# The start of a feed-forward stage in a hand-written order, two group sums in another group, and a two-factor multiply in the last norm

## The chip, the cores and the metric

The kernel runs on one core of a Trainium2 chip. The metric is device time in microseconds (us) of one execution; lower is better. All engines of the core (TensorE or PE, VectorE or DVE, ScalarE or ACT, GpSimd or POOL, and SyncE's queue SP for transfers) run side by side and wait for each other by semaphores.

## What is computed

One decoder block in float32 on 512 tokens of width 1024. The part that matters here is its second half:

```
x   = x + y @ W_out                              # 1024 x 1024
hm  = RMSNorm(x) * g_mlp
x   = x + relu(hm @ W1)**2 @ W2                  # W1 1024 x 4096, W2 4096 x 1024
out = RMSNorm(x) * g_final
```

Ahead of it stand a norm, an input projection, a pooling mixer, a latent attention with 8 heads and two gates. The change touches none of them.

## The kernel before

Every float32 matrix product is made of three matmuls on halves: an operand is cast by ScalarE to a rounded type (the high half, `hi`), VectorE subtracts that from the operand (the low half, `lo`), and TensorE adds hi*hi, hi*lo and lo*hi in PSUM. So each weight block costs a load, a ScalarE cast of 128x1024 and a VectorE subtraction of 128x1024 before TensorE can use it. Line 929 is the cast, line 932 the subtraction.

The feed-forward runs in four groups (`q` = 0 to 3) of 1024 hidden units. In each group both products are done in a form with seven block products where eight would be usual, at the price of sums and differences of blocks. In the "up" half (`up`, two halves `d` of 256 columns each) the seven block products are A11, S1, S2, A12, S3, S4 and A22, in this order on TensorE; S1 to S4 are running sums of weight blocks (`summed`, line 940). The tokens' side has the blocks B11, B21, B22 and the row forms T1 to T4, differences of blocks (`row_form`, lines 845 to 849, cast at line 1223, low half at line 1224). The results of S2 and S3 are copied to other PSUM banks before more is added (the forks `c` and `v`, line 1059; `b` at line 837 in group 0). ScalarE and VectorE then make relu squared and the forms of the hidden units (lines 1067 to 1092). In the "down" half (`down`) seven products, each in two steps, are added into the residual `xa` or into two kept sums, `U` and `V5` (line 1122). `U` and `V5` collect over groups 0 to 2 and are added to `xa` once, with eight VectorE additions of 128x512, at the end of `down` for group 2 (lines 1194 to 1201).

The order of all this is set by a small planner in the kernel's own Python (`emit_all`). Each operation has an engine, an assumed duration, the operations it needs, the buffers it takes, and a rank. The planner keeps an assumed clock for each engine (`free`). Time and again it takes, for each engine, the operations that could start within 0.2 us of the earliest one, chooses the one of lowest rank, and emits the choice that starts first. TensorE and SP take their lists strictly in order. On the chip each engine then runs its emitted list in order, and waits where an input is late. Weight blocks pass through five load buffers (`raw0` to `raw3` and `X`) and four pairs of hi and lo buffers.

Group 0 is special: its A11 and A12 are emitted by hand while W_out ends. The residual is norm'ed by 128-token tiles (`norm_rows`): tile 3 comes last, is transposed on TensorE into PSUM, and copied to `mT` (line 813), from which the row forms are made, for the first 128 columns of a block (`T[0, i]`) and for the last 128 (`T[1, i]`). In between, `early_forms` emits the weight sums S1 and S2 with their casts. Then the planner starts, from an assumed clock:

```python
    free.update(P=12.4, A=9.0, V=10.0)
    ...
    emit_all()
```

At the end the last norm squares each tile on ScalarE (`row_square`, line 1403), GpSimd raises the mean to the power -1/2 (line 1394), VectorE multiplies by `g_final` (lines 1427, 1428, 1443, 1446), and ScalarE (line 1410) or, for tile 3, VectorE (lines 1451, 1453) multiplies by the row's factor, half a row at a time, each half followed by its store on SP's queue. The last product's last tile is done in two halves of 256 columns.

Of the kernel before, what the change touches and what calls it, by code (L numbers as in the profile page):

```python
# [48 lines left out]
def block_kernel(ctx: ExitStack, tc: tile.TileContext, x, positions, g_mix, w_in, b_gate,  # L49
# [895 lines left out]
    def weights_up(q, d):  # L945
# [24 lines left out]
        rank_now[0] = step_of[K("S4")]  # L970
        s4 = summed(X("21"), X("21"), X("12"), p2 + [s3, ld["12"]])
        prepare(K("S4"), X("21"), [s4], 4)
        prepare(K("A22"), X("22"), [ld["22"]], 4)

# [32 lines left out]
    def up(q, d):  # L1007
# [25 lines left out]
        for n in UP_ORDER:  # L1033
# [19 lines left out]
            mm[n] = mm_op((q, d, n), UP_US, run, needs, (Bk[x],), (Bk[x],) if fresh else ())  # L1053
            if n in forks:
# [5 lines left out]
                fork_op[new] = use(act(512, copy, [mm[n]], step_of[q, d, n], (Bk[new],)), Bk[new], Bk[old])  # L1060
# [58 lines left out]
    given, r_op = [], {}  # L1119
# [7 lines left out]
    def down(q):  # L1127
# [158 lines left out]
    z = {n: [o for o in all_ops if o.tag == (0, 0, n)] for n in ("S1", "S2", "S3")}  # L1286
# [31 lines left out]
    def early_forms():  # L1318
        for o in z["S1"][1:] + z["S2"]:
            emit(o)  # L1320
# [47 lines left out]
    T = row_ops  # L1368
    def rows_then(*what):
        for o in what:  # L1370
            emit(o)
    rows_then(T[0, 0][0], T[0, 0][1], T[0, 1][0], T[0, 0][2], T[0, 1][1], T[0, 2][0], T[0, 1][2], T[0, 2][1], T[0, 3][0],
              T[0, 2][2], T[0, 3][1], T[0, 3][2])
# [4 lines left out]
    S3f = z["S3"]  # L1378
# [47 lines left out]
    for t in (0, 1):  # L1426
        nc.vector.tensor_mul(rows_o[t][0], xa[:, t, :], gf)
# [57 lines left out]
```

## Time and the profile before

| | |
|---|---|
| median of 3 runs | 684.94 us (684.65 to 686.38) |
| the profiled execution | 685.97 us |
| its span, first to last instruction | 684.2 us |
| TensorE busy, of the span | 663.0 us (97%) |
| VectorE, ScalarE, GpSimd busy | 516.0, 376.5, 83.2 us |
| mean granted TensorE clock | 0.991 of full speed |

The span is what the rows below are measured in; 1.77 us of the execution's own time lie around it. Times in rows count from the span's start. A timeline row gives start, duration, engine, line, operation, output<-input, shape and count; the square bracket at its end is how long the engine had been idle before it, and what ended the wait.

### The profile page before, as it was taken

To read this page: it belongs to the slowest core of one execution; us is meant where nothing else is said; L and a number is where in the kernel's file an instruction comes from. 1 tells how busy PE (TensorE), PEld (TensorE's weight loads), DVE (VectorE), ACT (ScalarE), POOL (GpSimd) and SP (SyncE) were. 2 spreads that over 40 slices of the span, in tenths; PEclk is the share of its full clock that TensorE was granted. 3 is DMA by queue.
4 is the path that set the end of the run, shared out by engine and by line. 5 is a ranking of instruction groups with operands and counts; after the bars stand their busy time and mean duration, and the time that the engine had idled before them with its cause. 6 is when DMAs were issued, how large, how long until landed. Compare 5 with 4: busy or idle time off the path is not lost.

```text
span 684.2 us, 9775 instructions
## 1 busy us (share of the span) xinstructions
PE 663.0 (97%) x3681; PEld 570.0 (83%) x3681; DVE 516.0 (75%) x793; ACT 376.5 (55%) x613; POOL 83.2 (12%) x101
## 2 busy tenths in 40 slices
PE   6999999999999999999998999999999999999994
PEld 3888888888888888888888977899889988899883
DVE  5767852478788764564579989788987989799996
ACT  4545252446655544442267784488535874368735
POOL 2216600000000000000000212002200022001212
PEclk8999999999999999999999999999999999999998
DMA  7423354642221125747504679338973398444953
GB/s 274 139 62 94 95 152 129 174 128 63 69 69 47 47 93 186 224 130 233 166 0 125 174 170 238 96 123 183 215 188 122 95 215 174 135 154 140 231 92 124
DMA packets 87047, 95.24 MB, mean 139 GB/s; under 512 B 6468, under 2 KB 61528, under 8 KB 87000
## 3 DMA queue, kind: packets, MB, share of 16 engines
q1 hardware_dynamic: 78296, 77.84, 36.1%
q0 software_dynamic: 8704, 16.78, 14.5%
q8 instruction: 29, 0.48, 0.3%
q14 instruction: 18, 0.15, 0.1%
HBM read 88.31 MB, written 6.29 MB: 138 GB/s over the span
## 4 chain that ended last, share of the span: by engine, by line
PE 89%; DVE 5%; ACT 2%; issue 1%; DMA 1%; POOL 0%; SPq 0%; POOLq 0%; DVEq 0%; ACTq 0%
PE P L777 7%; PE P L778 7%; PE P L776 7%; PE b L826 6%; PE a L826 5%; PE c L826 3%; PE v L826 3%; PE u L421 3%; PE lat L353 3%; PE e L826 2%; PE wo L777 2%; PE ga L71 2%; PE gb L70 2%; PE ga L70 2%; PE wo L776 2%; PE ga L72 2%
## 5 line engine op out<-in xcount | busy, mean ns | idle before, releaser
L929 ACT CAST xhi<-r_X 128x1024 fp32r<-128x1024 f32 x84 | 88.1, 1051 | 68.8 <-PE P L778 25.7
L932 DVE TENSOR_TENSOR xlo<-r_X,xhi 128x1024 fp32r<-128x1024 f32 x84 | 102.5, 1222 | 20.8 <-ACT xhi L929 20.3
L777 PE MATMUL P<-xlo,rhi 128*128 128x512 f32 (+1 forms) x228 | 89.5, 392 | 1.6 <-DVE xlo L932 1.5
L778 PE MATMUL P<-xhi,rlo 128*128 128x512 f32 (+1 forms) x228 | 89.1, 391 | 0.0
L776 PE MATMUL P<-xhi,rhi 128*128 128x512 f32 (+1 forms) x228 | 89.1, 391 | 0.0
L65 ACT CAST whi<-raw 128x1024 fp32r<-128x1024 f32 x45 | 46.7, 1050 | 45.4 <-PE bm L71 17.2
L66 DVE TENSOR_TENSOR wlo<-raw,whi 128x1024 fp32r<-128x1024 f32 x45 | 55.3, 1234 | 18.7 <-ACT whi L65 17.5
L777 PEld LDWEIGHTS P<-xlo,rhi 128*128 128x128 f32 x228 | 42.7, 187 | 12.7 <-DVE xlo L932 2.9
L776 PEld LDWEIGHTS P<-xhi,rhi 128*128 128x128 f32 x228 | 42.7, 187 | 10.0
L778 PEld LDWEIGHTS P<-xhi,rlo 128*128 128x128 f32 x228 | 42.7, 187 | 10.0
L915 POOL DMA_DIRECT2D r_X<-in_w_mlp_out x24 | 29.1, 1210 | 120.9 <-DVE xlo L932 116.6
L940 DVE TENSOR_TENSOR r_X<-r_X,r_X 128x1024 f32<-128x1024 f32 x32 | 39.1, 1223 | 5.0 <-DMA r_X<-in_w_mlp_in 4.5
L1081 DVE TENSOR_TENSOR rlo<-F,rhi 128x512 fp32r<-128x512 f32 x56 | 37.6, 687 | 6.9 <-ACT rhi L1078 6.8
L1078 ACT CAST rhi<-F 128x512 fp32r<-128x512 f32 x56 | 33.3, 620 | 1.0 <-DVE F L1087 0.5
L1122 DVE TENSOR_TENSOR xa<-xa,P 128x512 f32<-128x512 f32 (+1 forms) x53 | 33.0, 672 | 0.7 <-PE P L778 0.7
L665 ACT ACTIVATE p<-s,nm 128x128 f32<-128x128 f32 (+3 forms) x32 | 16.9, 528 | 19.9 <-DVE nm L662 19.4
L915 POOL DMA_DIRECT2D r_T<-in_w_mlp_out x8 | 9.7, 1213 | 145.3 <-ACT rhi L1078 49.5
L826 PE MATMUL a<-mb_hi,xhi 128*128 128x256 f32 x96 | 27.0, 281 | 0.0
L826 PE MATMUL a<-mb_hi,xlo 128*128 128x256 f32 x96 | 27.0, 281 | 0.0
L826 PE MATMUL a<-mb_lo,xhi 128*128 128x256 f32 x96 | 27.0, 281 | 0.0
L70 PE MATMUL gb<-h_hi,whi 128*128 128x512 f32 x64 | 26.4, 412 | 0.0
L71 PE MATMUL gb<-h_lo,whi 128*128 128x512 f32 x64 | 25.6, 400 | 0.0
(297 smaller groups left out, 1923.9 us busy)
## 6 DMA issues: line engine op xcount, KB each, us to landing
r_X<-in_w_mlp_in SPq DMA_DIRECT2D x32, 512.0 KB, 4.6
r_X<-in_w_mlp_out POOLq DMA_DIRECT2D x24, 512.0 KB, 6.5
raw<-in_w_in SPq DMA_DIRECT2D x20, 512.0 KB, 4.0
r<-in_w_mlp_out SPq DMA_DIRECT2D x16, 512.0 KB, 6.2
raw<-in_w_attn_proj SPq DMA_DIRECT2D x8, 512.0 KB, 3.5
raw<-in_w_out SPq DMA_DIRECT2D x8, 512.0 KB, 4.9
r_X<-in_w_mlp_out SPq DMA_DIRECT2D x8, 512.0 KB, 4.0
r_T<-in_w_mlp_out SPq DMA_DIRECT2D x8, 512.0 KB, 4.0
```

Source lines behind the costliest of these rows:

```text
L65: nc.scalar.copy(hi, src)
L66: (lo_eng or nc.vector).tensor_tensor(out=lo, in0=src, in1=f32(hi), op=ALU.subtract)
L70: nc.tensor.matmul(acc, whi, ahi, start=first, stop=False)
L71: nc.tensor.matmul(acc, whi, alo, start=False, stop=False)
L776: nc.tensor.matmul(acc, a_hi, w_hi, start=first, stop=False, skip_group_check=again)
L777: nc.tensor.matmul(acc, a_hi, w_lo, start=False, stop=False, skip_group_check=again)
L778: nc.tensor.matmul(acc, a_lo, w_hi, start=False, stop=last, skip_group_check=again)
L826: nc.tensor.matmul(acc[:, j, :], u[:, k, js], b[:, k, :], start=fresh and j + k + n == 0, stop=j == 1 and k == 3 and n == 2, skip_group_ch ...
L915: op = Op("G", ADD_US, lambda: nc.gpsimd.dma_start(buf.tile.rearrange("p (a b) -> p a b", a=a), src, accum_op=ALU.add), needs, rank_now[0])
L929: nc.scalar.copy(hi, buf.tile)
L932: lo_op = use(vec_op(1024, lambda: nc.vector.tensor_tensor(out=pb.tile[1], in0=buf.tile, in1=f32(pb.tile[0]), op=SUB), [hi_op], k), buf)
L940: return use(vec_op(1024, lambda: nc.vector.tensor_tensor(out=O.tile, in0=A.tile, in1=Bb.tile, op=op), needs, rank_now[0]), *{A, Bb, O})
```

## The change

Three edits. In the first, the start of group 0 is written out by hand. Only S2's sum stays in `early_forms`; its cast and low half, the forks, the row forms of both halves, the copies of the transposes, S3, S4, A22 and the first fork `c` get a written place on ScalarE and VectorE. The assumed clocks are set where the list starts and moved along. TensorE's own order stays as it was. In the second, the eight additions of `U` and `V5` get the rank `rk(6)` of group 2 instead of a rank eight steps into group 3. In the third, tiles 1 and 2 of the last norm are multiplied by `g_final` and the row's factor in one VectorE instruction; tile 3's first stored half is scaled by ScalarE instead of VectorE.

```diff
     def weights_up(q, d):
...
         rank_now[0] = step_of[K("S4")]
+        tag_now[0] = K("S4")
         s4 = summed(X("21"), X("21"), X("12"), p2 + [s3, ld["12"]])
         prepare(K("S4"), X("21"), [s4], 4)
+        tag_now[0] = None
+        tag_now[0] = K("A22")
         prepare(K("A22"), X("22"), [ld["22"]], 4)
+        tag_now[0] = None
...
         if q == NG - 2:
-            k = first_step[NG - 1]
+            k = rk(6)
             for t in range(2):
-                vec_op(512, lambda t=t: add(C[2, 0][:, t, :], keep_sum["U"][:, t, :]), u6, k + 8)
-                o = vec_op(512, lambda t=t: add(keep_sum["V5"][:, t, :], keep_sum["U"][:, t, :], SUB), u6 + v5, k + 8)
+                vec_op(512, lambda t=t: add(C[2, 0][:, t, :], keep_sum["U"][:, t, :]), u6, k)
+                o = vec_op(512, lambda t=t: add(keep_sum["V5"][:, t, :], keep_sum["U"][:, t, :], SUB), u6 + v5, k)
                 for r in (1, 2):
-                    vec_op(512, lambda r=r, t=t: add(C[r, 1][:, t, :], keep_sum["V5"][:, t, :]), [o], k + 8)
+                    vec_op(512, lambda r=r, t=t: add(C[r, 1][:, t, :], keep_sum["V5"][:, t, :]), [o], k)
...
     def early_forms():
-        for o in z["S1"][1:] + z["S2"]:
+        for o in z["S1"][1:] + z["S2"][:1]:
             emit(o)
...
         up_mm(up_w[0, d, "A11"], "B11", banks[0, d, "a"], fresh=True)
-        fork(0, d, "b", "a")
+    T, S3f = row_ops, z["S3"]
...
+    free.update(A=3.5, V=4.6)
+    fork(0, 0, "b", "a")
+    then(T[0, 0][0], T[0, 0][1], z["S2"][1], T[0, 2][0], T[0, 1][0], T[0, 0][2])
+    late = []
+    for half in range(2):
+        pt = psT.tile([P, 4, P], F32, name=f"n2pt3_{half}", tag="T")
+        for j in range(4):
+            k = half * 4 + j
+            nc.tensor.transpose(pt[:, j, :], hrow[3][:, k * P:(k + 1) * P], ident)
+        late.append((slice(half * 4, half * 4 + 4), slice(3 * P, 4 * P), pt))
+    keep_rows(late)
+    fork(0, 1, "b", "a")
+    free["A"] = max(free["A"] + 1.8, 8.0)
+    then(z["S2"][2], S3f[0], T[0, 1][1], T[1, 0][0], T[1, 0][1], T[0, 1][2], T[1, 0][2])
+    for d in range(2):
+        up_mm(up_w[0, d, "A12"], "B21", banks[0, d, "a"])
...
-    keep_rows(transpose_norm(3))
-    for d in range(2):
-        up_mm(up_w[0, d, "A12"], "B21", banks[0, d, "a"])
-    free.update(P=12.4, A=9.0, V=10.0)
-    rows_then(T[1, 0][0], T[1, 0][1], T[1, 1][0], T[1, 0][2], T[1, 1][1], S3f[0], T[1, 1][2], S3f[1], T[1, 2][0], S3f[2],
-              T[1, 2][1], T[1, 3][0], T[1, 2][2], T[1, 3][1], T[1, 3][2])
-    norm.close()
+    then(T[0, 2][1], T[1, 1][0], T[1, 1][1], T[0, 2][2], T[1, 1][2], S3f[1], T[1, 2][0], T[1, 2][1], S3f[2], T[1, 2][2],
+         z["S4"][0])
+    hi, lo = (v[:, :, P:] for v in M["B22"])
+    split(late[1][2], hi, lo)
...
+    free["P"] = 12.4
+    free["A"] += 1.2
+    free["V"] += 0.7
+    then(named[0, 0, "S1"], named[0, 0, "S2"], named[0, 0, "c"], z["S4"][1], T[0, 3][0], T[0, 3][1], T[1, 3][0], z["S4"][2],
+         T[1, 3][1], T[0, 3][2], T[1, 3][2], *z["A22"])
+    norm.close()
...
-    room["raw"].append((0.0, "X"))
+    room["raw"].append((free["V"], "X"))
...
+    def row_out(o, t, cs):
+        nc.vector.scalar_tensor_tensor(out=o[:, cs], in0=xa[:, t, cs], scalar=rows_r[t], in1=gf[:, cs],
+                                       op0=ALU.mult, op1=ALU.mult)
+        send(o, t, cs)
...
-    for t in (0, 1):
-        nc.vector.tensor_mul(rows_o[t][0], xa[:, t, :], gf)
-    nc.vector.tensor_mul(fo3[:, 512:], xa[:, 3, 512:], gf[:, 512:])
-    row_out(0)
-    square3(0, slice(512, 1024))
-    row_out(1)
+    square3(0, halves[1])
+    nc.vector.tensor_mul(fo[0], xa[:, 0, :], gf)
+    nc.vector.tensor_mul(fo3[:, halves[1]], xa[:, 3, halves[1]], gf[:, halves[1]])
+    for cs in halves:
+        nc.scalar.activation(fo[0][:, cs], fo[0][:, cs], AF.Copy, scale=rows_r[0])
+        send(fo[0], 0, cs)
...
             row_square(2)
-            nc.vector.tensor_mul(rows_o[2][0], xa[:, 2, :], gf)
-    row_out(2)
+            for cs in halves:
+                row_out(fo[1], 1, cs)
     v = small.tile([P, 1], F32, name="fv3", tag="fv3")
+    row_out(fo[2], 2, halves[0])
     nc.vector.tensor_reduce(out=v, in_=ms3, axis=AX.X, op=ALU.add)
     r = rstd_end(v, nc.vector)
-    nc.vector.tensor_scalar_mul(fo3[:, 512:], fo3[:, 512:], r)
-    nc.sync.dma_start(out[3 * P:, 512:], fo3[:, 512:])
-    nc.vector.tensor_scalar_mul(fo3[:, :512], fo3[:, :512], r)
-    nc.sync.dma_start(out[3 * P:, :512], fo3[:, :512])
+    row_out(fo[2], 2, halves[1])
+    nc.scalar.activation(fo3[:, halves[1]], fo3[:, halves[1]], AF.Copy, scale=r)
+    send(fo3, 3, halves[1])
+    nc.vector.tensor_scalar_mul(fo3[:, halves[0]], fo3[:, halves[0]], r)
+    send(fo3, 3, halves[0])
```

## Rows read from the trace of the kernel before

**Rows 1.** The page, part 1: busy time of the engines in us, share of the span, instructions.

```profile
PE 663.0 (97%) x3681; PEld 570.0 (83%) x3681; DVE 516.0 (75%) x793; ACT 376.5 (55%) x613; POOL 83.2 (12%) x101
```

**Rows 2.** Busy time by stretch (start:end, length, then busy time of PE, its weight loads, DVE, ACT and POOL with instruction counts, granted clock, DMA share, GB/s).

```profile
373.00:411.00 38.00, 36.01 (x239) 31.99 (x237) 33.83 (x42) 31.43 (x48) 6.24 (x5) 1.00 0.71 180
411.60:600.00 188.40, 188.40 (x1163) 168.09 (x1162) 161.54 (x185) 112.54 (x147) 22.78 (x19) 1.00 0.66 161
583.00:600.00 17.00, 17.00 (x98) 14.75 (x97) 13.90 (x17) 6.90 (x7) 0.00 (x0) 1.00 0.36 115
600.00:622.00 22.00, 20.88 (x174) 20.49 (x173) 21.39 (x25) 16.35 (x24) 0.00 (x0) 1.00 0.44 140
640.00:684.20 44.20, 35.09 (x163) 28.55 (x161) 35.20 (x50) 20.63 (x32) 8.89 (x11) 0.94 0.56 140
```

**Rows 3.** TensorE's timeline in the feed-forward, matmuls on either side of its waits.

```profile
355.11 0.28 PE L826 MATMUL a<-mb_hi,wlo 128*128 128x256 f32 x1
...
355.61 0.63 PE L803 MATMUL n2pt<-ident,n2h 128*128 128x128 f32 x4 [0.22 <-DVE n2h L133]
...
362.31 0.28 PE L826 MATMUL a<-mb_hi,wlo 128*128 128x256 f32 x1
...
364.35 0.39 PE L826 MATMUL e<-t_lo,xhi 128*128 128x256 f32 x1 [0.36 <-DVE t_lo L1224]
...
369.90 0.28 PE L826 MATMUL b<-t_hi,xlo 128*128 128x256 f32 x1
...
371.01 0.39 PE L826 MATMUL c<-t_hi,xhi 128*128 128x256 f32 x1 [0.84 <-ACT c L1059]
...
385.20 0.28 PE L826 MATMUL b<-t_hi,xlo 128*128 128x256 f32 x1
...
386.14 0.39 PE L826 MATMUL c<-t_hi,xhi 128*128 128x256 f32 x1 [0.66 <-ACT c L1059]
...
404.01 0.50 PE L777 MATMUL P<-xlo,rhi 128*128 128x512 f32 x1 [0.47 <-DVE xlo L932]
...
411.27 0.50 PE L777 MATMUL P<-xlo,rhi 128*128 128x512 f32 x1 [1.06 <-DVE xlo L932]
...
621.66 0.39 PE L826 MATMUL b<-t_hi,xlo 128*128 128x256 f32 x1 [1.12 <-DVE xlo L932]
```

**Rows 4.** The chain of work that ended last, in order of time (start, us, what): the first product of group 3.

```profile
594.50 2.84 PE a L826 x24
```

**Rows 5.** Timeline of VectorE, then of GpSimd with the transfers that it issues, then of SP's queue, around the start of the feed-forward.

```profile
348.40 1.23 DVE L940 TENSOR_TENSOR r_X<-r_X,r_X 128x1024 f32<-128x1024 f32 x1
350.79 1.23 DVE L932 TENSOR_TENSOR xlo<-r_X,xhi 128x1024 fp32r<-128x1024 f32 x1 [1.17 <-ACT xhi L929]
351.94 0.68 DVE L1340 TENSOR_TENSOR xa<-xr,wo 128x512 f32<-128x512 f32 x1
...
354.72 1.41 DVE L133 SCALAR_TENSOR_TENSOR n2h<-xa,n2r,g 128x512 f32<-128x512 f32 x2 [0.67 <-POOL n2r L90]
...
354.13 0.55 POOL L90 TENSOR_TENSOR n2r<-n2v,neghalf 128x1 f32<-128x1 f32 x1 [8.35 <-DVE n2v L88]
...
388.57 2.45 POOL L915 DMA_DIRECT2D r_T<-in_w_mlp_out  x2 [0.82 <-DMA r_T<-in_w_mlp_out]
...
367.81 4.62 SPq L909 DMA_DIRECT2D r_X<-in_w_mlp_in  x4
```

**Rows 6.** Groups of instructions by line (engine, operation, shapes, count | busy us, mean ns of one | idle before and what ended it): a weight block's cast, and a row form's low half.

```profile
L929 ACT CAST xhi<-r_X 128x1024 fp32r<-128x1024 f32 x84 | 88.1, 1051 | 68.8 <-PE P L778 25.7 <-DMA r_X<-in_w_mlp_out 24.4 <-DVE r_X L940 5.2
...
L1224 DVE TENSOR_TENSOR t_lo<-tf,t_hi 128x512 fp32r<-128x512 f32 x8 | 5.5, 688 | 0.2
```

**Rows 7.** VectorE's timeline at the end of group 2 and the start of group 3.

```profile
586.25 1.23 DVE L940 TENSOR_TENSOR r_X<-r_X,r_X 128x1024 f32<-128x1024 f32 x1 [3.07 <-DMA r_X<-in_w_mlp_in]
587.39 1.28 DVE L1122 TENSOR_TENSOR U<-U,P 128x512 f32<-128x512 f32 x2
...
590.32 1.22 DVE L932 TENSOR_TENSOR xlo<-r_X,xhi 128x1024 fp32r<-128x1024 f32 x1
...
592.06 1.28 DVE L1122 TENSOR_TENSOR xa<-xa,P 128x512 f32<-128x512 f32 x2
...
607.33 1.28 DVE L1122 TENSOR_TENSOR xa<-xa,V 128x512 f32<-128x512 f32 x2
```

**Rows 8.** Timeline of the last norm: VectorE, ScalarE, GpSimd, and the last store on SP's queue.

```profile
670.39 2.36 DVE L1427 TENSOR_TENSOR fo<-xa,gf 128x1024 f32<-128x1024 f32 x2
...
675.92 0.41 DVE L1122 TENSOR_TENSOR xa<-xa,P 128x256 f32<-128x256 f32 x1
...
675.08 1.32 ACT L1410 ACTIVATE fo<-fo,fr 128x512 f32<-128x512 f32 x2
...
677.74 0.40 ACT L1421 ACTIVATE fjunk<-xa 128x256 f32<-128x256 f32 x1
...
671.78 1.40 POOL L1394 TENSOR_TENSOR fr<-fr,neghalf 128x1 f32<-128x1 f32 x1
...
673.58 0.57 POOL L1394 TENSOR_TENSOR fr<-fr,neghalf 128x1 f32<-128x1 f32 x1
...
678.70 0.55 POOL L1394 TENSOR_TENSOR fr<-fr,neghalf 128x1 f32<-128x1 f32 x1 [0.29 <-DVE fr L1393]
...
680.72 0.42 SPq L1454 DMA_DIRECT2D out<-fo  x1
```

More of the change, by code (lines that the diff above doesn't have):

```diff
@@ L1052, in up @@
                 needs.append(row_op[form])
-            mm[n] = mm_op((q, d, n), UP_US, run, needs, (Bk[x],), (Bk[x],) if fresh else ())
+            mm[n] = named[q, d, n] = mm_op((q, d, n), UP_US, run, needs, (Bk[x],), (Bk[x],) if fresh else ())
             if n in forks:
@@ L1059, in copy @@
                     nc.scalar.copy(Bk[new].tile, Bk[old].tile)
-                fork_op[new] = use(act(512, copy, [mm[n]], step_of[q, d, n], (Bk[new],)), Bk[new], Bk[old])
+                fork_op[new] = named[q, d, new] = use(act(512, copy, [mm[n]], step_of[q, d, n], (Bk[new],)), Bk[new], Bk[old])
         mmx = lambda n: [mm[n]] if n in mm else []
@@ L1118, in block_kernel @@
     SS4 = 99
-    given, r_op = [], {}
+    given, r_op, named = [], {}, {}
     def add(dst, src, op=ALU.add):
@@ L1284, in emit @@
                 room[b.kind].append((b.end, b.name) if b.kind == "raw" else b.end)
-    z = {n: [o for o in all_ops if o.tag == (0, 0, n)] for n in ("S1", "S2", "S3")}
+    z = {n: [o for o in all_ops if o.tag == (0, 0, n)] for n in ("S1", "S2", "S3", "S4", "A22")}
     bufs_of, users_key = {}, {}
@@ L1364, in block_kernel, with then @@
         up_mm(up_w[0, d, "A11"], "B11", banks[0, d, "a"], fresh=True)
-        fork(0, d, "b", "a")
+    T, S3f = row_ops, z["S3"]
+    def then(*what):
+        for o in what:
+            emit(o)
+    free.update(A=3.5, V=4.6)
[8 more added lines that the diff above has]
+        late.append((slice(half * 4, half * 4 + 4), slice(3 * P, 4 * P), pt))
@@ L1366, in block_kernel @@
+    keep_rows(late)
[4 more added lines that the diff above has]
+        up_mm(up_w[0, d, "A12"], "B21", banks[0, d, "a"])
     for b, (d, x) in zip(given, ((0, "a"), (0, "b"), (1, "a"), (1, "b"))):
         b.tile = banks[0, d, x]
[L1368 to L1373, printed above, removed]
@@ L1374, in block_kernel @@
-    keep_rows(transpose_norm(3))
-    for d in range(2):
-        up_mm(up_w[0, d, "A12"], "B21", banks[0, d, "a"])
-    free.update(P=12.4, A=9.0, V=10.0)
-    S3f = z["S3"]
-    rows_then(T[1, 0][0], T[1, 0][1], T[1, 1][0], T[1, 0][2], T[1, 1][1], S3f[0], T[1, 1][2], S3f[1], T[1, 2][0], S3f[2],
-              T[1, 2][1], T[1, 3][0], T[1, 2][2], T[1, 3][1], T[1, 3][2])
-    norm.close()
+    then(T[0, 2][1], T[1, 1][0], T[1, 1][1], T[0, 2][2], T[1, 1][2], S3f[1], T[1, 2][0], T[1, 2][1], S3f[2], T[1, 2][2],
+         z["S4"][0])
@@ L1396, in rstd_end @@
         return r
-    rs, rows_o = [], {}
+    rs, rows_r = [], {}
     def row_square(t):
@@ L1403, in row_square, with row_tile, send @@
         nc.scalar.activation(junk, xa[:, t, :], AF.Square, scale=1.0 / math.sqrt(D), accum_out=ms)
-        rows_o[t] = wp.tile([P, D], F32, name=f"fo{t}", tag=f"raw{(t + 1) % 4}", bufs=1), rstd_end(ms)
-    def row_out(t):
-        o, r = rows_o[t]
-        for c in range(2):
-            cs = slice(c * 512, (c + 1) * 512)
-            nc.scalar.activation(o[:, cs], o[:, cs], AF.Copy, scale=r)
-            nc.sync.dma_start(out[t * P:(t + 1) * P, cs], o[:, cs])
+        rows_r[t] = rstd_end(ms)
+    def row_tile(t):
+        return wp.tile([P, D], F32, name=f"fo{t}", tag=f"raw{(t + 1) % 4}", bufs=1)
+    halves = [slice(c * 512, (c + 1) * 512) for c in range(2)]
+    def send(o, t, cs):
+        nc.sync.dma_start(out[t * P:(t + 1) * P, cs], o[:, cs])
+    def row_out(o, t, cs):
+        nc.vector.scalar_tensor_tensor(out=o[:, cs], in0=xa[:, t, cs], scalar=rows_r[t], in1=gf[:, cs],
+                                       op0=ALU.mult, op1=ALU.mult)
+        send(o, t, cs)
     one, p2 = ends
@@ L1416, in block_kernel @@
     ms3 = small.tile([P, 3], F32, name="fms3", tag="fms3")
+    fo = [row_tile(t) for t in range(3)]
     fo3 = wp.tile([P, D], F32, name="fo3", tag="raw0", bufs=1)
```

## The prediction, made before the changed kernel was run

> **What bounds the kernel.** I read the page first, then busy time by stretch, then TensorE's timeline where a stretch falls short of full, and last the other engines' timelines there. The page gives TensorE 97% of the span [rows 1]: what can be won is TensorE's idle time and the tail behind its last matmul. Between 411.6 and 600 it is busy for all 188.4 us [rows 2]; no edit gains there. The waits stand in four places. At the start of the feed-forward TensorE stops for tile 3's norm and for the row form T1, then for the fork `c` [rows 3]. Early in group 0's down half it stops twice for a weight block's low half, and once more in group 3 at 621.66 [rows 3]. After TensorE's last work comes the last norm; the stretch from 640 holds 9.1 us without a matmul (44.20 less 35.09) [rows 2]. VectorE is the engine that makes it wait: from 600 to 622 it is busy for 21.39 of 22.00 us [rows 2].
>
> **First edit, start of group 0.** Before, VectorE sums S2 at 348.40, then does S2's low half at 350.79, and only then adds tile 3's residual at 351.94 [rows 5]. With the low half moved behind, the addition starts when the sum ends, near 349.6, that is 2.3 us earlier, and square, GpSimd's power and the two-factor multiply follow by as much: the tile is ready at 353.8 instead of 356.13 [rows 5]. TensorE is then still in A11, so the wait of 355.61 goes: 0.50 from start to start where 0.12 is the pace (24 matmuls in 2.84 [rows 4]), worth 0.38 [rows 3].
>
> S1 waits for T1's second half. From 362.31 to the low half's matmul at 364.35 lie 2.04 us in which two steps of 0.12 belong; 1.80 is lost [rows 3]. In the new order VectorE has, between tile 3's norm and T1's last low half, seven operations of 128x512 and two of 128x1024. At 0.64 (two in 1.28) and 1.14 (586.25 to 587.39) [rows 7] that is 6.8 us, so T1 is ready near 360.6. TensorE gets there at 362.05, so S1 doesn't wait, with 1.4 us to spare; only if VectorE were held that long by ScalarE's casts would the 1.80 begin to come back.
>
> The fork `c` can't start before S2 ends, and S3 can't before the fork. For `d` = 1, where ScalarE was free for it, this cost 0.94 from start to start; for `d` = 0 it cost 1.11 [rows 3]. Emitted by hand ahead of S4's cast it should cost the lower: 0.17 gained. What queues behind the waiting copy on ScalarE is S4's cast, and VectorE waits for that: copy done at 368.6, cast 1.05 [rows 6], low half 1.23, so 370.9, where TensorE wants S4 at 371.01 - 2.35 + 2.84 = 371.5. That is the tightest link, 0.6 us. The four weight loads for `d` = 1 go out on SP from 367.81, as buffers come free [rows 5]; S3's and S4's sums, which free the first two, come earlier in the new list, so the loads start no later. No work is removed; what moves is hidden by TensorE's 5.7 us in A12. Sum: 0.38 + 1.80 + 0.17 = 2.35 (at least 1.9, if the spare time is half eaten; at most 2.5).
>
> **What that does to the rest of group 0.** TensorE comes 2.35 us earlier to the work that VectorE finishes at the old time: by 373 both orders have done the same set on VectorE. From 373 to 411 VectorE is busy 33.83 of 38.00 us [rows 2], so 4.2 us are free, more than the lead. The waits at 404.01 and 411.27 (0.47 and 1.06 [rows 3]) come after VectorE itself has idled, with a low half queued behind other work: a mismatch between planner and chip. Before, the planner's VectorE clock stood at 10.0 where its TensorE clock said 12.4; TensorE was there at 362.4, so VectorE's clock meant 360.0, while T1's last low half was still awaited at 364.3 [rows 3]. The new clocks (A = 3.5, V = 4.6 at the list's head) mean 353.0 and 354.1, and the tile comes at 353.8: they fit. I take 1.1 of the 1.5 us. Upper end 1.5. Lower end -0.7: S2 of `d` = 1 could be late by that much if VectorE kept the old times.
>
> **Second edit, the eight additions.** `rk(6)` of group 2 is 79, the old rank was 88, group 3's A11 has 80 and S1 81 (52 and 80 being the groups' first steps). The planner takes the lowest rank among what can start, so the eight additions now go ahead of A11's and S1's low halves. VectorE waits 3.07 us for a load at 586.25, which the planner didn't foresee, or the additions to `U` would not stand behind it; then come `U`, one low half, and, at 592.06, two additions to `xa`; A11's low half was at 590.32 [rows 7]. In the new order two plus eight additions of 0.6 stand between 589.7 and that low half: it starts at 595.7 and ends near 596.9. TensorE begins A11 at 594.50 [rows 4] and needs it 0.24 later: a wait of 2.2 us. On the other side six of the eight leave the full stretch before 621.66 (the last pair was at 607.33 [rows 7]), and its 1.12 goes. Full price -1.1. If the additions instead fall into the 3.07 us, 583 to 600 having 3.1 us free in all [rows 2], TensorE doesn't wait and 1.1 is gained. I take -0.7, nearer the end that the ranks give; down to -1.6 if S2's low half is late as well.
>
> **Third edit, the last norm.** ScalarE loses the four half-row scalings of tiles 1 and 2 and gains one of tile 3. The last quarter's square stood at 677.74 though its addition was done at 676.33, because ScalarE was in tile 1's scalings until 676.4 and in tile 2's square after [rows 8]. Without them the squares come about 1.0 earlier. VectorE gets four two-factor multiplies of 0.70 (two took 1.41 [rows 5]) in place of two multiplies of 1.2; two of them stand ahead of tile 3's additions and one ahead of the final sum, which takes back 0.4. That leaves 0.6 until the last power.
>
> GpSimd's power took 1.40 at 671.78, while VectorE ran the two multiplies of 670.39, and 0.57 and 0.55 where VectorE read PSUM or nothing [rows 8]. In the new order a two-factor multiply on VectorE starts beside the last power, and is half as long as those of 670.39, so I charge 0.3 for it (from nothing to 0.85, the difference of the rows), and put 0.2 on the other side for the first power, which has one multiply less beside it. The tail gains 0.6 - 0.3 + 0.2 = 0.5, with ends -0.2 (0.6 less the full 0.85) and 1.0 (nothing taken back). The Trainium skill says in "SBUF — State Buffer", Who interferes with whom, that a VectorE instruction with two inputs in SBUF holds a port that GpSimd's reads need, for its whole length. By that rule the last power would wait out the multiply's whole 0.70, the tail would gain 0.1, and the sum below would be 0.4 less; the three rows agree with the rule's direction.
>
> **Sum.** 2.35 + 1.1 - 0.7 + 0.5 = 3.25 us. The profiled execution took 685.97 with a span of 684.2; it should become 682.7. The median of the runs is 1.03 below the profiled one, so 684.94 becomes 681.7. All best ends together: 2.5 + 1.5 + 1.1 + 1.0 = 6.1, 678.8. All worst: 1.9 - 0.7 - 1.6 - 0.2 = -0.6, 685.5.
>
> **Rivals.**
> A, chance 0.17: the additions fill VectorE's free time before 590 and the planner's better clock removes nearly all waits: 2.35 + 1.5 + 1.1 + 0.5 = 5.45, so 679.5. For it: 3.1 us free before 600. Against: the load that VectorE waits for stands first.
> B, chance 0.19: the lead is handed back in group 0. The third product's blocks need two loads in a row; GpSimd issues its adding load at 388.57 after the first has landed [rows 5], and at 404.01 TensorE waits for such a block's low half [rows 3]. If the buffers come free no earlier, TensorE waits there for what it won: -0.7 + 0.5, so 685.1, no change. Against: buffers free up with S3 and S4, which come earlier.
> C, chance 0.08, slower: the planner's choices shift in groups 1 to 3, where TensorE doesn't wait at all before 600. Four pairs of weight buffers turn over all the time; one allocation out of step costs what 404.01 and 411.27 did, 1.5 us with two per group. If each of the three groups catches that at both the up and the down half, 9.0 less 3.25 makes 690.7; it is slower than before from the third such pair of waits on. Against: before, the planner was off by 2 to 3 us in group 0 and at 586, and 188 us passed without a wait.
> D, chance 0.08: the additions cost their full 1.6 and the tail gives nothing: 2.35 + 1.1 - 1.6 = 1.85, so 683.1.
>
> **Numbers.** My forecast has 0.48, for 680.3 to 682.9. A measurement of this kernel tells about 0.3%, 2.05 us, from no change, so faster means below 682.89. Faster: the forecast's 0.46, A's 0.17, 0.02 of D: 0.65. Slower than 686.99: C's 0.07. The rest, 0.28, is the same. The range 679.0 to 685.2 leaves out A's lower part and most of C, some 2 in 10.
>
> **What would show it.** Right: no wait of TensorE at the transposes and S1, `c` at 0.66 idle, the new S3 start near 368.7; a wait at group 3's A11 for VectorE near 594, none at S2 of its second half; the last store issued about 0.5 earlier behind the last matmul. Wrong: TensorE waiting for T1, S4 or the third product's blocks in group 0, or anywhere in groups 1 and 2; no wait at A11 of group 3; a last power over 1 us long.

## The result, and the profile after

The change made the kernel slower. In 20 executions each, the kernel after took 688.61 us in the median (684.15 to 692.22), the kernel before 684.52 us (682.41 to 686.38); the ratio is 1.0049, with a 95% interval of 1.0031 to 1.0068, so 3.4 us are lost (2.1 to 4.7), where 3.25 were to be won.

The profiled execution of the kernel after is one of its shorter ones: 686.24 us, span 684.4 us, 2.4 us below the median. Its page, part 1, beside [rows 1], shows as much work as before:

```profile
PE 662.1 (97%) x3681; PEld 569.8 (83%) x3681; DVE 515.6 (75%) x794; ACT 374.2 (55%) x610; POOL 83.6 (12%) x101
```

Busy time by stretch, the columns and stretches of [rows 2]:

```profile
373.00:411.00 38.00, 33.20 (x207) 28.70 (x206) 32.57 (x41) 30.99 (x46) 6.33 (x6) 1.00 0.72 172
411.60:600.00 188.40, 187.48 (x1157) 167.12 (x1156) 163.07 (x190) 111.41 (x145) 22.20 (x19) 1.00 0.66 163
583.00:600.00 17.00, 16.08 (x91) 13.78 (x90) 16.01 (x21) 6.88 (x7) 0.00 (x0) 1.00 0.35 121
600.00:622.00 22.00, 21.42 (x179) 21.01 (x178) 19.26 (x19) 16.45 (x23) 0.00 (x0) 1.00 0.38 120
640.00:684.20 44.20, 35.19 (x162) 28.35 (x160) 35.16 (x52) 19.98 (x30) 9.35 (x11) 0.96 0.57 142
```

TensorE's free time grew from 1.99 to 4.80 us between 373 and 411, and from nothing to 0.92 between 411.6 and 600. VectorE is busier before 600 (16.01 of 17.00 where it had 13.90) and freer behind (19.26 where it had 21.39): the additions did move. TensorE's timeline, the waits that answer to [rows 3]:

```profile
366.98 0.39 PE L826 MATMUL c<-t_hi,xhi 128*128 128x256 f32 x1 [0.71 <-ACT c L1063]
...
376.20 0.38 PE L826 MATMUL e<-t_hi,xlo 128*128 128x256 f32 x1 [0.21 <-DVE xlo L932]
...
379.87 0.39 PE L826 MATMUL b<-t_hi,xhi 128*128 128x256 f32 x1 [0.80 <-ACT xhi L929]
...
381.13 0.39 PE L826 MATMUL b<-t_hi,xlo 128*128 128x256 f32 x1 [0.76 <-DVE xlo L932]
...
384.67 0.38 PE L826 MATMUL c<-t_hi,xhi 128*128 128x256 f32 x1 [0.66 <-ACT c L1063]
...
401.34 0.50 PE L777 MATMUL P<-xlo,rhi 128*128 128x512 f32 x1 [1.88 <-DVE xlo L932]
...
410.46 0.50 PE L777 MATMUL P<-xlo,rhi 128*128 128x512 f32 x1 [0.48 <-DVE xlo L932]
...
594.85 0.39 PE L826 MATMUL a<-mb_hi,xlo 128*128 128x256 f32 x1 [0.92 <-DVE xlo L932]
...
621.51 0.39 PE L826 MATMUL b<-t_hi,xlo 128*128 128x256 f32 x1 [0.53 <-DVE xlo L932]
...
653.36 0.50 PE L777 MATMUL P<-xlo,rhi 128*128 128x512 f32 x1 [0.60 <-DVE xlo L932]
```

The waits for tile 3 and for T1 are gone. New are those at S2 of `d` = 1 (0.80 and 0.76, with 0.21 at S1), at group 3's A11 (0.92) and in group 3's down half (0.60); the third product's in group 0 grew from 0.47 to 1.88. The two waits at 411.27 and 621.66 became shorter, 0.48 and 0.53.

The start of the feed-forward lies anywhere between 346.40 and 348.88 us in the profiles shown here, also where the code ahead of it is the same. So the profiles are laid on each other at the transposes of tile 2, before and then after:

```profile
348.67 1.03 PE L803 MATMUL n2pt<-ident,n2h 128*128 128x128 f32 x8
```

```profile
347.32 1.03 PE L803 MATMUL n2pt<-ident,n2h 128*128 128x128 f32 x8
```

The lead is how much earlier a point stands than before, once these two rows are laid on each other:

| TensorE's timeline | before | after | lead |
|---|---|---|---|
| S3 of group 0, `d` = 0 | 371.01 | 366.98 | 2.68 |
| first matmul of group 0's down half | 394.75 | 393.29 | 0.11 |
| group 1's A11 | 436.34 | 435.53 | -0.54 |
| group 3's A11 | 594.33 | 593.52 | -0.54 |
| group 3's S1 | 597.17 | 597.55 | -1.73 |
| group 3's down half | 635.73 | 635.58 | -1.20 |
| last matmul | 674.82 | 675.51 | -2.04 |
| end of the span | 684.2 | 684.4 | -1.55 |

So the first edit's lead is made as forecast and is gone before the down half; then 1.2 us go at group 3's A11 and 0.8 in the last down half. A second profiled execution of the same kernel (`after_again`, 688.91 us, near the median) lost 4.6 where this one lost 1.55: 0.7 more up to group 1 and 2.5 more at group 3's A11. The second edit's experiments say why for the larger part.

### The profile page after: what moved, and what is told of

Read it like the earlier page. It is cut to its first block, busy times and chain, and to the rows that moved or that the text cites. A ratio compares the mean times of both kernels' runs of the same rounds, so it can differ in the third digit from the quotient of the medians.

```text
span 684.4 us, 9769 instructions
## 1 busy us (share of the span) xinstructions
PE 662.1 (97%) x3681; PEld 569.8 (83%) x3681; DVE 515.6 (75%) x794; ACT 374.2 (55%) x610; POOL 83.6 (12%) x101
## 4 chain that ended last, share of the span: by engine, by line
PE 75%; DVE 9%; DMA 7%; ACT 5%; issue 3%; POOL 0%; SPq 0%; POOLq 0%; ACTq 0%; DVEq 0%
PE a L826 5%; PE b L826 4%; DVE xlo L932 4%; PE P L777 4%; PE P L778 4%; PE P L776 4%; PE u L421 3%; PE lat L353 3%; DVE xa L1126 2%; ACT xhi L929 2%; PE wo L777 2%; PE gb L70 2%; PE ga L72 2%; PE ga L70 2%; PE ga L71 2%
```

## The experiments

**Each edit by itself, and the whole change once more.** Theory 1: what the first edit gains is lost again in group 0. Theory 2: the second edit costs more than it was charged, at group 3's A11. The edits were put singly on the kernel before. The first is the hand-written start, cut to its core:

```diff
...
+    free.update(A=3.5, V=4.6)
+    fork(0, 0, "b", "a")
+    then(T[0, 0][0], T[0, 0][1], z["S2"][1], T[0, 2][0], T[0, 1][0], T[0, 0][2])
...
-    free.update(P=12.4, A=9.0, V=10.0)
...
```

> The first edit alone. Theory 1 (the loss sits in group 0's later part): ratio to the kernel before above 1.003, about +3 to +5 us, spread over several us from run to run as with the whole change (684 to 692), with TensorE's lead of 2.7 us at S3 gone by the first down product, and a wait of 2 us or more at the third product's blocks. Theory 2 (the loss sits at group 3's A11, from the additions): ratio below 0.998, about 1 to 2.5 us faster, runs within 1.5 us of each other.

The second:

```diff
-            k = first_step[NG - 1]
+            k = rk(6)
...
-                vec_op(512, lambda t=t: add(C[2, 0][:, t, :], keep_sum["U"][:, t, :]), u6, k + 8)
+                vec_op(512, lambda t=t: add(C[2, 0][:, t, :], keep_sum["U"][:, t, :]), u6, k)
...
```

> The second edit alone. Theory 1: within 0.2% of the kernel before; a wait of about 1 us at group 3's first A11, and the 1.1 us at the second half's S2 gone or halved. Theory 2: 3 to 5 us slower, with the run-to-run spread of the whole change.

The third:

```diff
+        nc.vector.scalar_tensor_tensor(out=o[:, cs], in0=xa[:, t, cs], scalar=rows_r[t], in1=gf[:, cs],
+                                       op0=ALU.mult, op1=ALU.mult)
...
```

> The third edit alone. Both theories: 0.3 to 0.7 us faster (ratio 0.9990 to 0.9996), the last power near 1 us long instead of 0.55, everything before 669 us unchanged.

All three, as changed:

> The whole change once more, for a profile of another execution. Theory 1: if this execution is one of the longer ones, the extra time shows as a longer wait of TensorE in group 0 at the third product's blocks (behind GpSimd's adding loads), with a lower granted clock after it. Theory 2: it shows at group 3's A11 or after.

Measured, each as a ratio to the kernel before on the same chip: first edit 1.0001 (0.9989 to 1.0012), second 1.0045 (1.0026 to 1.0063), third 0.9983 (0.9968 to 0.9998), all 1.0046 (1.0029 to 1.0064). In us that is 0, 3.1 lost (1.8 to 4.3) and 1.2 won (0.1 to 2.2). Theory 2 holds for the loss. The first edit comes to nothing, which neither theory had. The three by themselves add up to 1.9 lost, the whole change loses 3.1 to 3.4; the difference is within the intervals.

TensorE's timeline with the second edit alone, at group 3's A11 (690.43 us, one of its longer executions):

```profile
593.76 0.28 PE L826 MATMUL a<-mb_hi,xhi 128*128 128x256 f32 x1
593.88 0.28 PE L826 MATMUL a<-mb_lo,xhi 128*128 128x256 f32 x1
596.95 0.38 PE L826 MATMUL a<-mb_hi,xlo 128*128 128x256 f32 x1 [2.78 <-DVE xlo L932]
597.17 0.28 PE L826 MATMUL a<-mb_hi,xhi 128*128 128x256 f32 x1
...
598.12 0.41 PE L826 MATMUL a<-mb_hi,xhi 128*128 128x256 f32 x1
598.34 0.41 PE L826 MATMUL a<-mb_lo,xhi 128*128 128x256 f32 x1
...
601.05 0.28 PE L826 MATMUL a<-mb_hi,xlo 128*128 128x256 f32 x1
601.18 0.28 PE L826 MATMUL e<-t_hi,xhi 128*128 128x256 f32 x1
```

VectorE's timeline of the same execution:

```profile
585.93 1.23 DVE L940 TENSOR_TENSOR r_X<-r_X,r_X 128x1024 f32<-128x1024 f32 x1 [3.14 <-DMA r_X<-in_w_mlp_in]
...
589.40 0.69 DVE L1122 TENSOR_TENSOR xa<-xa,U 128x512 f32<-128x512 f32 x1
...
594.46 1.29 DVE L1122 TENSOR_TENSOR xa<-xa,V 128x512 f32<-128x512 f32 x2
595.67 1.22 DVE L932 TENSOR_TENSOR xlo<-r_X,xhi 128x1024 fp32r<-128x1024 f32 x1
```

And its busy time by stretch, with the granted clock as third number from the end:

```profile
592.00:598.00 6.00, 3.22 (x18) 2.64 (x17) 5.96 (x10) 1.30 (x2) 0.00 (x0) 0.96 0.27 99
598.00:604.00 6.00, 6.00 (x41) 6.00 (x41) 4.64 (x5) 1.53 (x2) 0.00 (x0) 0.75 0.04 16
```

The additions hold A11's low half until 595.67, and TensorE waits 2.78. Soon after it runs on, a matmul takes 0.21 instead of 0.12 from start to start (598.12 to 598.34), until about 600.9: the lower of its two clock levels, 1.2 instead of 2.4 GHz. The Trainium skill says in "TensorE: Matmul & The Clock Gate", Part 1, that the array's clock is halved when it has been idle; these rows agree in direction, but not every wait of such a size is followed by the lower clock (last section). The block takes 7.42 us instead of 2.84: 2.95 go at the wait (3.07 from start to start in place of 0.12), the other 1.6 to the clock. Against that, S2 of the second half no longer waits (1.1 back), but the down half of group 3 has a new wait of 1.17 at 656.82, behind four additions of results that stand ahead of the low half in the new order.

How long A11 waits depends on when the load for VectorE's sum lands, the wait in front of 585.93: from that sum to the start of A11's low half VectorE is almost never idle and takes 9.73 or 9.74 us in all three profiles. The sum began 9.68 before A11 in the profile after, 8.67 in the repetition and 7.83 here; the waits were 0.92, 1.94 and 2.78, the blocks 4.03, 6.58 and 7.42 us long. In the first the clock stayed up. The three executions took 686.24, 688.91 and 690.43 us, so this is a likely reason why the executions of the kernel after lie so far apart; for the others it isn't shown. Their mean granted clocks fit (of the twenty, those up to 686.24 us have 0.991 to 0.995, those from 688.05 on 0.988 to 0.991) but don't prove it: the mean also holds stretches at the lower clock early in the kernel and behind the last matmul, and in the repetition's runs 685.81 us has 0.990 and 688.22 us 0.993.

**First and third edit without the second** (the change, with the second diff above undone).

> First and third edit, second edit undone. If the second edit is the whole loss (additions ahead of group 3's A11 low half), this is norm_only's time again: about 683.4, ratio 0.998 to the kernel before, no wait over 0.5 at group 3's first A11, the second half's S2 waits 1.1 again at about 621, and the spread of runs falls back to some 3 to 4 us. If the loss came from the parts meeting (start edit together with the others), the ratio stays above 1.002.

683.63 us, ratio 0.9986 (0.9973 to 1.0000): within its interval the third edit's own. No wait at group 3's A11; the 1.1 at S2 behind it, which was expected back, isn't in its profile either. The loss belongs to the second edit; on top of the other two it costs about 4.2 us.

**The first edit without the third product's adding loads.** This kernel leaves out the part of the sum that those two loads add, so only its time says something.

```diff
-                    prepare((q, h, n), (q, h, n), [load((q, h, n), src, 2, Bq[h]["22"] if n == "T3" else None)], 2)
+                    prepare((q, h, n), (q, h, n), [load((q, h, n), src, 2, Bq[h]["22"] if n == "T3" and q else None)], 2)
```

> First edit alone, and in group 0 the third product's factor is taken without the two GpSimd loads that add the second part onto it (that part of the sum is left out). If those adding loads, which start after the first load has landed, hand the lead back, the wait of 1.8 at about 402 in front of the down product goes, and group 1 starts about 1.5 to 2 us earlier against the transposes than before does; the time is about 682.8, ratio 0.9975. If the lead is lost earlier (S2 of the second half, 0.8 and 0.8) or to the buffers of loads, group 1 starts at most 0.5 earlier and the ratio is 1.000.

682.27 us, ratio 0.9961 (0.9945 to 0.9976): as expected if those loads are to blame, and group 1's A11 leads by 2.39. But the way there is not the one expected. At the first matmul of the down half the lead was already down to 0.33, as in the other runs with the first edit so far (-0.21, 0.11, 0.32). The down half then took 39.53 us where the first edit alone needs 42.00 and the kernel before 41.59; the waits at 404.01 and 411.27, which the kernel before also has, went. So with the first edit the loads cost the down half 2.5 us. That they are behind these waits in the kernel before too is likely, not shown: there the cast of the third product's second block starts at 400.52, right behind the landing of its adding load at 400.44, but no run took the loads out of that kernel. The lead itself is lost in the up half. ScalarE's timeline with the first edit alone, the cast that those loads hold up:

```profile
398.92 1.05 ACT L929 CAST xhi<-r_T 128x1024 fp32r<-128x1024 f32 x1 [2.39 <-DMA r_T<-in_w_mlp_out]
```

The same cast without the adding loads:

```profile
396.47 1.03 ACT L929 CAST xhi<-r_T 128x1024 fp32r<-128x1024 f32 x1
```

**The low half's passes last in each up block, with the second edit.**

```diff
+        for passes in ((0, 1), (2,)):
...
-                for n, (u, b) in enumerate(((whi, bhi), (whi, blo), (wlo, bhi))):
...
+                    for n in passes:
...
```

> Second edit alone, and in every block of the up products the passes with the low half of the weight come after the passes with the high half, instead of being mixed in; the additions stand where the second edit puts them. If the loss is TensorE waiting in the middle of group 3's A11 block for its late low half, the first two thirds of the block (about 1.9 us) now run ahead of it: the wait falls from 2.8 to 1.0 or less, the granted clock between 592 and 604 stays at 1.00, and the ratio to before falls from 1.0045 to 0.998 to 1.001. If it is contention (VectorE's additions against TensorE) or later buffers, the order of passes changes nothing: 1.003 or more.

687.67 us, ratio 1.0052 (1.0035 to 1.0069): not the gain of the first case, but the "1.003 or more" of the second. The profiled execution, its longest (693.45), shows the wait at the new place, behind the passes with the high half:

```profile
599.90 2.07 PE L828 MATMUL a<-mb_hi,xlo 128*128 128x256 f32 x8 [2.67 <-DVE xlo L934]
```

The passes did run ahead, from 595.17 on. But VectorE's sum had to wait for its load until 588.90, 6.27 before A11 where it was 7.83, so the low half came 1.6 us later against TensorE, and the clock fell to 0.59 between 598 and 604. Whether the order of passes itself makes the loads later wasn't separated from chance. This run decides nothing between the theories.

**The additions between the two places.**

```diff
-                vec_op(512, lambda t=t: add(C[2, 0][:, t, :], keep_sum["U"][:, t, :]), u6, k + 8)
+                vec_op(512, lambda t=t: add(C[2, 0][:, t, :], keep_sum["U"][:, t, :]), u6, k + 2)
...
```

> The eight additions at rank 82 instead of 79 or 88: the planner then puts them behind A11's low half but ahead of the sum and the low half of S1. By VectorE's rows S1's low half starts near 600.3 instead of 595.65, so the wait leaves A11 (0.3 or less) and appears at S1, about 4 us long. If a wait costs its own length, the time rises by 4 less the 1.1 saved at the second half: about 687.4, ratio 1.004. If a long wait also takes the granted clock down for the matmuls behind it, a loss of 5 to 8 us: ratio 1.007 to 1.012, with the clock below 0.9 between 597 and 606. If where the additions stand does not matter for the path, 1.000.

688.56 us, ratio 1.0053 (1.0033 to 1.0073). The expectation misread one row: the low half behind the additions is S2's, not S1's, which is done before them. In the profiled execution (686.59, one of the shorter) S2 waits 0.29 and 0.76 near 599, the down half 0.87 at 652.06, and the clock stays at 1.00. Its tail behind the last matmul is 10.52 us instead of 9.38, for a reason given below (work for TensorE during the wait). What the longer executions lose isn't in this profile. It shows only that this place is no better.

**The additions in VectorE's idle time,** ahead of the sum that waits for its load, with the third edit.

```diff
...
-        s1 = summed(X("21"), X("21"), X("22"), [ld["21"], ld["22"]])
+        s1 = summed(X("21"), X("21"), X("22"), [ld["21"], ld["22"]] + (group_adds if q == NG - 1 and d == 0 else []))
...
-            k = first_step[NG - 1]
+            k = rk(4)
...
```

> Third edit, and the eight additions (with the two to U ahead of them) put in front of S1's first sum in group 3, so that VectorE does them while that sum's load is still on its way. In the profile of the third edit alone VectorE idles 3.35 us there, from 581.85 to 585.20, and U's product was finished by about 582. If VectorE's free time is what the additions lacked, the sum starts some 3 us later than the load allows instead of the additions standing behind it, A11 waits at most 0.5, the 1.1 at the second half's S2 goes, and the time is 682.3 to 682.8, ratio 0.9965 to 0.997. If the late low half is only handed on to S1 or S2 of the first half (the chain has some 0.5 us to spare there by the rows), a wait of 0.8 to 1.5 appears at about 599 and the time is 684 to 686, ratio 0.999 to 1.002.

683.45 us, ratio 0.9980 (0.9969 to 0.9991), the third edit's own and between the two cases expected. VectorE's timeline, between the last low half before the wait and the sum:

```profile
581.96 1.22 DVE L932 TENSOR_TENSOR xlo<-r_X,xhi 128x1024 fp32r<-128x1024 f32 x1 [1.79 <-ACT xhi L929]
583.10 1.28 DVE L1122 TENSOR_TENSOR U<-U,P 128x512 f32<-128x512 f32 x2
584.30 0.69 DVE L1122 TENSOR_TENSOR xa<-xa,U 128x512 f32<-128x512 f32 x1
...
588.15 1.29 DVE L1122 TENSOR_TENSOR xa<-xa,V 128x512 f32<-128x512 f32 x2
...
592.83 1.22 DVE L940 TENSOR_TENSOR r_X<-r_X,r_X 128x1024 f32<-128x1024 f32 x1
```

All eight additions are done by 589.4, also ahead of A11's low half, and A11 doesn't wait. The sum now stands behind two low halves, A11's among them, so nothing that A11 needs waits for its load. So it is not the additions before A11 that cost the 3 us, but their place behind an operation that waits for a load. The wait at S2 of the second half (1.19 with the third edit alone) is gone; at S2 of the first half TensorE waits 0.56, where the third edit alone has 0.46. Laid on the transposes, this profile ends 1.25 us earlier than the third edit's, but the ratios of the runs (0.9980 and 0.9983) show no such gain; where it goes in the other executions stays open.

**The additions later.** Third edit, `k + 8` made `k + 20`.

```diff
-                vec_op(512, lambda t=t: add(C[2, 0][:, t, :], keep_sum["U"][:, t, :]), u6, k + 8)
+                vec_op(512, lambda t=t: add(C[2, 0][:, t, :], keep_sum["U"][:, t, :]), u6, k + 20)
...
```

> Third edit, and the eight additions 12 ranks later than before instead of 9 earlier. If they are what makes S2 of group 3's second half late, that wait of 1.2 at about 621 goes and nothing else appears, since VectorE has 1.3 us free between 624 and 640 and 8.9 after it: 682.3, ratio 0.9965. If VectorE is full there, the wait moves to another block and the ratio stays at 0.998 to 1.000.

684.82 us, ratio 1.0009 (0.9995 to 1.0024). The wait at 621 went, as expected, and the gain didn't come: by the ratios this order is some 1.8 us slower than the third edit alone, with intervals that just overlap. The profiled execution (683.47) shows where the gain goes. It has a new wait of 0.35 at 649.57, for an addition to `xa`. Laid on the transposes, its last matmul still comes 1.16 us earlier than the third edit's, but VectorE's work doesn't come earlier with it: the tail behind the last matmul takes 9.77 us instead of 8.31.

**Work for TensorE during the wait,** with the second edit: what part of the loss is the clock?

```diff
+                if (q, d, n) == (NG - 1, 0, "A11"):
+                    for i in range(16):
+                        nc.tensor.matmul(Bk[x].tile[:, 0, :], pair_tile[q, d, n][0][:, i % 4, :P], M[form][0][:, i % 4, :],
+                                         start=True, stop=True, skip_group_check=True)
```

> Second edit alone, with 16 more matmuls of 128x256 put ahead of group 3's A11 (high half by high half, into the bank that A11 then overwrites; they add nothing to the result and take 16 x 0.118 = 1.9 us). TensorE needs the low half 1.9 us later, so its wait falls from 2.8 to about 0.9. If waits cost only their own length, the time is the same as with the additions alone, within 0.5 us: 687.5 to 688.5, ratio 1.0045. If the granted clock falls because TensorE stood idle, the clock stays at 1.00 from 592 to 604 in most executions and 1.4 to 1.7 us come back: 686.5 to 687, ratio 1.002 to 1.003, in spite of 1.9 us more work.

TensorE's timeline at A11, and the busy time by stretch:

```profile
593.53 2.06 PE L1045 MATMUL a<-mb_hi,xhi 128*128 128x256 f32 x16
595.43 0.28 PE L826 MATMUL a<-mb_hi,xhi 128*128 128x256 f32 x1
595.54 0.27 PE L826 MATMUL a<-mb_lo,xhi 128*128 128x256 f32 x1
596.83 0.39 PE L826 MATMUL a<-mb_hi,xlo 128*128 128x256 f32 x1 [1.01 <-DVE xlo L932]
...
599.53 0.28 PE L826 MATMUL e<-t_hi,xhi 128*128 128x256 f32 x1
```

```profile
592.00:598.00 6.00, 4.99 (x36) 4.47 (x35) 5.97 (x10) 1.08 (x2) 0.00 (x0) 1.00 0.26 96
598.00:604.00 6.00, 5.96 (x51) 5.75 (x50) 5.89 (x6) 2.23 (x4) 0.00 (x0) 1.00 0.03 12
```

In this execution it went as the clock theory says: the low half came 2.0 us after A11's turn, as with the additions alone, the wait is 1.01, the clock stays at 1.00, and extra work and block together take 6.00 us where the block alone took 7.42. The median doesn't follow: 689.23 us, ratio 1.0069 (1.0052 to 1.0087), no gain and rather a loss. The filling takes its 1.9 us in every execution, also where the wait would have been shorter, and the clock need not fall in every one. And the profiled execution ends with a longer tail, 10.5 us behind the last matmul where the additions alone have 9.7. There GpSimd's first operation of the last norm, on one number per row, lasts 2.28 us, beside VectorE's multiplies by `g_final`:

```profile
673.95 2.28 POOL L1397 TENSOR_SCALAR fr<-fms 128x1 f32<-128x1 f32 x1 [9.96 <-ACT fjunk L1407]
```

With the additions alone it takes 0.53 and the power behind it 1.40 instead of 0.57. So ScalarE gets the first row's factor 0.85 later against the last matmul, about what the tail is longer by. The two other kernels with the same tail, 10.52 (the low half's passes last and the additions between, both above), have the same long operation. So the fall of the clock adds to the price where it occurs; its share of the median loss stays open.

**Low passes last, without the second edit.** In every up block as above, and in the down blocks too; once with the third edit alone, once with the first as well, once with the third edit and the additions in the idle time.

```diff
+                    for i, (r, w) in enumerate(((r_hi, w_hi), (r_lo, w_hi), (r_hi, w_lo))):
+                        for t in range(2):
+                            for j in (0, 1):
...
```

> Third edit, additions as before, and in every block of the up and the down products the passes with the weight's low half come last. Waits for a low half that are under 1.9 us in an up block and 0.9 in a down block are covered by the other passes: those of 0.5 and 1.1 in group 0's down half and of 1.1 in group 3 go, 2.3 us less the third edit's own time: 681 to 682, ratio 0.995. If low halves are late because buffers of weights come free late (they are now held to the end of each block), the loads shift by as much and the ratio stays at 0.998.

> First and third edit with the low passes last. If the first edit's lead of 2.4 us is lost only to low halves that come up to 1.9 late, it is kept now: 679.5 to 681, ratio 0.993. If it is lost to the loads of the third product, whose second load can't start before the first has landed, 682 to 683.5 as for the first and third edit alone.

> Third edit, low passes last in every block, and the eight additions in front of S1's sum in group 3. If both remedies act on different waits, the 1.1 to 1.5 that is left at 611 to 621 goes as well: 679 to 680.5, ratio 0.9935 to 0.995. If the additions only hand the lateness on, 680.5 to 682 as with the low passes last alone.

In this order: 680.65 us, ratio 0.9960 (0.9941 to 0.9979); 681.75 us, ratio 0.9953 (0.9934 to 0.9972); 681.84 us, ratio 0.9960 (0.9947 to 0.9974). All three beat both kernels, by some 3 us the one before, and can't be told apart. Each is faster than the kernel that differs from it in the order of passes alone (0.9983, 0.9986 and 0.9980), by 1.4 to 2.3 us; the intervals of the single pairs overlap or just miss each other, but the three agree. The two profiles without the first edit fit: the waits at 404.01 and 621.66 are gone, that at 411.27 is 0.46 and 0.49 instead of 1.06. The first of them, one of its longer executions (684.20), has a new wait of 1.49 for the fork `v` at 611.12.

The first edit's lead again adds nothing that can be measured, but its profile tells more about the loss: at the first matmul of the down half 1.23 us of the lead are left, where the first and third edit with the old order of passes have 0.32. So about 0.9 of the 2.4 us lost up to there go to late low halves. The other 1.5 go to S2's cast (a wait of 1.19), and in the down half more than the rest is lost against the same kernel without the first edit (group 1's A11 leads by 0.95, and by 1.70 without the first edit). The additions in the idle time bring nothing more, as the second case said.

## Why the prediction was wrong

**First edit, start: right.** 2.35 was forecast (at most 2.5), 2.68 came, in the profile after and with the first edit alone (367.97 less 348.31 against 371.01 less 348.67: 2.68). The waits named went, and `c` idles 0.71 where 0.66 was said. The rest of the difference is 0.26 that was won between tile 3's transposes and A12, which the sum didn't have.

**Rest of group 0: the step that failed first.** Forecast was 1.1 more; the lead was lost whole, so that the first edit is worth 0 instead of 3.45. The step read "4.2 us are free, more than the lead". VectorE's free time was not where it was needed. VectorE's timeline before, then after:

```profile
373.17 1.22 DVE L940 TENSOR_TENSOR r_X<-r_X,r_X 128x1024 f32<-128x1024 f32 x1
...
376.99 2.49 DVE L940 TENSOR_TENSOR r_X<-r_X,r_X 128x1024 f32<-128x1024 f32 x2
```

```profile
367.92 1.23 DVE L932 TENSOR_TENSOR xlo<-r_X,xhi 128x1024 fp32r<-128x1024 f32 x1 [1.63 <-ACT xhi L929]
...
371.40 1.22 DVE L940 TENSOR_TENSOR r_X<-r_X,r_X 128x1024 f32<-128x1024 f32 x1
...
376.18 2.49 DVE L940 TENSOR_TENSOR r_X<-r_X,r_X 128x1024 f32<-128x1024 f32 x2
```

VectorE stands for 1.63 us for S4's cast, which stands behind the fork `c`. The prediction saw that queue, found S4 itself in time by 0.6, and didn't ask what VectorE does behind it. Laid on the transposes, the sum at 371.40 comes 0.4 earlier than before, and those at 376.18, S2 of `d` = 1 among them, 0.5 later. TensorE came 2.7 earlier and waited. The lower end named this place ("if VectorE kept the old times") and gave it 0.7; with S1 just ahead of it, it took 2.6 here and 2.4 to 2.9 in the other profiles. That VectorE's wait causes it is read from the rows; no run took that wait away. With the low passes last 1.5 was lost there. The 1.1 itself was to come from the waits at 404.01 and 411.27, which the text put down to a mismatch of planner and chip. Without the adding loads both are gone, so with the first edit it is those loads, rival B's third product, that set them: the cast for it waits 2.4 to 2.6 us for the adding loads, which take 11.2 us on average from issue to landing where they took 9.8.

**Second edit: the mechanism right, the price wrong, and that decided the sign.** The arithmetic put A11's low half at 595.7 and the wait at 2.2; with the additions alone it stood at 595.67 and the wait was 2.78. The first figure fits so well by luck: laid on the transposes it is 596.35. The wait at 621.66 went, as said (0.53 of it stayed in the kernel after). Three things failed. The text computed a full price of -1.1 and then took -0.7, on the chance that the additions fill idle time; they stood behind the waiting sum in every profile of the second edit. It priced the wait by its length; the matmuls behind it ran at the lower clock for some 3 us in that profile. And it left out what the planner makes of the rest of group 3: a wait of 0.60 to 1.17 in its down half in every profile of the second edit. Charged 0.7, measured 3.1 by itself (about 4.2 on top of the other two). How the 3.1 of the median splits into the wait, the clock and the down half isn't measured.

**Third edit: right in sign, by other terms.** Forecast 0.5; the profiled tail behind the last matmul went from 9.38 to 8.88, and to 8.31 with the third edit alone, whose ratio gives 1.2 (0.1 to 2.2). The last power, charged 0.3, took 0.99 instead of 0.55. GpSimd's and VectorE's timelines after:

```profile
678.89 0.99 POOL L1415 TENSOR_TENSOR fr<-fr,neghalf 128x1 f32<-128x1 f32 x1 [1.36 <-DVE fr L1414]
```

```profile
678.73 0.74 DVE L1437 SCALAR_TENSOR_TENSOR fo<-xa,fr,gf 128x512 f32<-128x512 f32 x1
```

They overlap by 0.58 us and the power is 0.44 longer than [rows 8] had it. Up to the power's start 0.50 was won against the last matmul (0.6 forecast), so by its end nearly nothing was left. What the text didn't count comes behind it, where both halves of tile 3 are now scaled side by side:

```profile
679.91 0.72 ACT L1483 ACTIVATE fo<-fo,fr 128x512 f32<-128x512 f32 x1 [1.93 <-POOL fr L1415]
```

```profile
679.91 0.49 DVE L1485 TENSOR_SCALAR fo<-fo,fr 128x512 f32<-128x512 f32 x1 [0.44 <-POOL fr L1415]
```

From the power's end to the span's end it is 4.50 us instead of 4.95. The Trainium skill's rule ("SBUF — State Buffer", Who interferes with whom) agrees with the longer power in direction, though the power lost 0.44 and not the whole 0.58 of the overlap; the tail of 0.1 worked out from it lacked the same gain.

**The rivals.** B (lead handed back, no change, 0.19) was right for the first edit, though mostly at another place. D named the second edit's loss, at half its size. C, the only slower one, expected waits in groups 1 to 3, at both the up and the down half of each. From 436 to 594, in groups 1 and 2, TensorE again waits for nothing; in group 3 both came, but through the rank of the additions and not by a shift of buffers. The range ended at 685.2 because its worst ends were too near zero: -0.7 for group 0, where the lead could be lost whole, and -1.6 for the additions.

## What to carry to other kernels

A move that puts operations behind one that waits for a transfer is priced from when the transfer lands, on the chip and not in the plan: ask what stands behind the waiting operation, and by how much its next consumer is early. A lead on one engine is worth what the engine that feeds it can also move forward; free time counts only after that engine's last wait. Where the low or late operand is one of several, let the passes that don't need it go first: here that was worth some 1.4 to 2.3 us with the additions at a place where they don't hold A11 up, while with the second edit it gained nothing.

## What was not expected of the hardware

A wait of TensorE of 1.80 us in group 0 was followed by full speed in one execution and by the lower clock in another. Busy time from 400 to 406 with the first edit alone, where the wait ends at 402.40:

```profile
400.00:406.00 6.00, 4.20 (x18) 3.11 (x17) 5.34 (x7) 5.88 (x10) 0.00 (x0) 1.00 0.78 173
```

The same stretch of the kernel after, repeated, where it ends at 400.58:

```profile
400.00:406.00 6.00, 5.42 (x17) 4.29 (x18) 5.68 (x8) 5.97 (x10) 0.17 (x1) 0.72 0.74 194
```

So one wait has two prices, its own length or some 1.6 us more (so much the clock took at group 3's A11, in the repetition and with the second edit alone), and which it is can't be read from its length: a wait of 1.88 in the profile after was followed by full speed too.
